# Sparse-expert stage on Trainium2: experts of two kinds taken in turn, with down products one expert behind

## The chip, the cores and the metric

The kernel runs on one core of a Trainium2 chip. The metric is the device time in microseconds (us) of one execution; several executions are timed and their median counts. A profile, taken by the hardware profiler, covers one execution.

The engines are PE (TensorE, matrix products; PEld is its loading of weights, which runs beside the products), DVE (VectorE), ACT (ScalarE), POOL (GpSimd) and SP (SyncE, which here issues most of the transfers).

## What is computed

A decoder of two layers for 256 tokens of 1024 channels in float32. Layer 1 ends with a SwiGLU of eight experts, of which each token uses two; the change lies there:

```python
logits = (xt @ w_router).astype(jnp.float32)
top_val, top_idx = lax.top_k(logits, TOP_K)          # 2 of 8
gates = jax.nn.softmax(top_val, axis=-1)
...
def expert_block(args):
    xb, e = args
    g, u = jnp.split(xb @ w_gate_up[e], 2, axis=-1)  # 1024 -> 2 x 3584
    return (jax.nn.silu(g) * u) @ w_down[e]          # 3584 -> 1024
```

The expert's rows, times their gates, are added to the residual. After it come a gated per-layer embedding and a last norm. The weights of one expert are 28 MiB for gate and up and 14 MiB for down, 44.04 MB in all; those of all eight, 352 MB, pass through once.

## The kernel before

**Precision.** A float32 product is made of products of two reduced parts: the high part of a tile is a copy in PE's reduced format, the low part the remainder. Every weight tile of 1 MiB that arrives is split so in two halves of 128 x 1024 by `wsplit`: ACT casts the high part `h_...` (line 145), DVE subtracts it and so makes the low part `l_...` (line 146). There are four buffers for each of the two (`SPL_BUFS`). `split` (lines 197 and 198) does the same for activations. All products are issued by `mm` (line 174).

**Two kinds of experts.** On the chip the experts are ranked by their number of tokens. The first four (ranks 0 to 3) have 128 slots: high and low tokens are separate tiles, and each piece of weights is used in three products of 512 columns, six for a half. The last four (`few(e)`, `FEW = 4`) have 64 slots: the high and low parts of their tokens stand side by side in one tile of 128 columns, so two products do, four for a half. Before, rank 0 comes first and rank 7 last.

**Chunks.** An expert's 3584 inner columns are taken in four chunks (`CHUNKS`), three of 1024 and one of 512. For each, `gate_up` makes the gate and up values in PSUM (`mg`, `mu`). `activate`, which `gate_up` returns, empties PSUM: for 128 slots ACT's Silu and DVE's product make the SwiGLU tile `msg` (lines 1191 and 1192); for 64 slots ACT copies both (`msg`, `msu`, line 1188). `h_T` then turns each tile of 512 columns on PE, since `down` needs the inner dimension on partitions: 128 slots by four transposes (line 1220) and a split into `mhh` and `mhl`; 64 slots by 16 small products with `both`, which add the low half to the high one at the same time (`mt`), after which Silu and product (lines 1211 and 1212) make `mgu` and a split makes `mh`. `down` adds the chunk's share to `y` in PSUM; after an expert's last chunk `combine` multiplies `y` with the slots' matrix and adds it to the residual `h` with the gates (line 1249).

**Order.** The loop at the end takes expert after expert and chunk after chunk. It issues `gate_up` of a chunk, then `back` of the chunk before. `h_T` of the chunk before is issued inside `gate_up`, at its second k tile (`MID = 1`), and `activate` of the present chunk after half of the `down` products (`between`). A scheduler fixes each engine's order from this order of issue; an engine then works strictly in its order. `gather` collects the tokens of two 128-slot experts, or of the four 64-slot ones, by products with a one-hot matrix; `spread_slots` turns that matrix for `combine`.

**Transfers.** Weights are requested on SP's queue in the order of use, into a ring of 11 buffers of 1 MiB (`raw`, `RAW_BUFS`; lines 766, 769 and 167), and for the first of them into two spare pairs of buffers (`SPARE`). A request waits until DVE has split what the buffer held. The weights of the last block (`r_dl`, line 1264) are split by output halves, so that the norm behind the stage can begin with the first half.

Of the kernel before, what the change touches and what calls it, by code (L numbers as in the profile page):

```python
# [16 lines left out]
P = 128  # L17
# [66 lines left out]
def trunk_kernel(  # L84
# [18 lines left out]
    def s2(name, shape, dt=F32):  # L103
        return ar.tile(list(shape), dt, tag="s2", name=name, bufs=S2_BUFS)

# [3 lines left out]
    def pt(name, shape=(P, 512)):  # L109
        return ps.tile(list(shape), F32, tag="t", name=name, bufs=2)  # L110
# [62 lines left out]
    def mm(o, a, b, start, stop, shared=False):  # L173
        last["mm"] = pe.matmul(o, a, b, start=start, stop=stop, skip_group_check=shared)  # L174
# [28 lines left out]
    def sub2(pr, *idx):  # L203
        return pr[0][idx], pr[1][idx]
# [738 lines left out]
    def layer1_moe(pT):  # L943
# [110 lines left out]
        def few(e):  # L1054
            return e >= FEW

# [141 lines left out]
        def h_T(e, c, sgs):  # L1198

            res = []  # L1200

            for i, sg in enumerate(sgs):
                if few(e):

                    q = pt(f"mt{e}{c}{i}", (P, 2, 4, P // 2))
                    for j in range(2):
                        for g in range(2):
                            for k in range(2):
                                mm(q[:, j, 2 * g + k, :], sg[j][:, 256 * g + k : 256 * g + 256 : 2], both, True, True)
                    t = s2(f"mgu{e}{c}{i}", [P, 4, P // 2])  # L1210
                    act.activation(t, q[:, 0], AF.Silu)
                    dve.tensor_tensor(t, q[:, 1], t, MUL)
                    hT = s2(f"mh{e}{c}{i}", [P, 4, 2, P // 2], F32R)
                    split((hT[:, :, 0], hT[:, :, 1]), t)
                    res += [hT[:, k].rearrange("q i s -> q (i s)") for k in range(4)]
                    continue
                q = pt(f"mt{e}{c}{i}", (P, 4, P))
                for g in range(2):
                    for k in range(2):
                        pe.transpose(q[:, 2 * g + k, :], sg[:, 256 * g + k : 256 * g + 256 : 2], ident)  # L1220
                hT = (s2(f"mhh{e}{c}{i}", [P, 4, P], F32R), s2(f"mhl{e}{c}{i}", [P, 4, P], F32R))
                split(hT, q)
                res += [sub2(hT, slice(None), k) for k in range(4)]
            return res

        def down(e, c, hT, yb, between):

            c0, n = CHUNKS[c]
            res = None
            for g in range(n // 256):  # L1230
# [3 lines left out]
                for i in range(2):  # L1234
                    products(e, [(yb[half], hT[2 * g + i], sub2(wt[i], slice(None), HALF[half])) for half in range(2)],
                             c == g == i == 0, c == len(CHUNKS) - 1 and g == n // 256 - 1 and i == 1)
                if g == n // 512 - 1 and between:
                    res = between()
            return res

        def combine(e, yb, half):
            s = slice(half * 512, half * 512 + 512)
# [8 lines left out]
        yb, hT = {}, {}  # L1251
        both = sm("both", (P, P // 2))
        dve.tensor_tensor(both, ident[:, : P // 2], ident[:, P // 2 :], ADD)

        def back(e, c, between=None):
            if c == 0:
                yb[e] = [py(f"y{e}{half}") for half in range(2)]
            if (e, c) == (NE - 1, len(CHUNKS) - 1):
                part = hT.pop((e, c))
# [11 lines left out]
            res = down(e, c, hT.pop((e, c)), yb[e], between)  # L1271
            if c == len(CHUNKS) - 1:
                for half in range(2):
                    combine(e, yb[e], half)
            return res

        def more_slots(e, pos):

# [58 lines left out]

            return over > P, more

        prev = None  # L1340
        for e in range(NE):
            for c in range(len(CHUNKS)):
                if e % 2 == 1 and c == 2 and e <= FEW - 1:
                    spread_slots = gather(e // 2 + 1)
                if (e, c) == (FEW, 1):
                    spread_slots()

                def mid():
                    if prev:
                        hT[prev] = h_T(*prev, sg)  # L1350
                    if (e, c) == (0, LATE):
                        for bn in todo:
                            product(*bn, pt)
                            copy(*bn)

                activate = gate_up(e, c, mid)
                if prev:
                    sg = back(*prev, activate)
                else:
                    sg = activate()  # L1360
                    with after("wsplit"):
                        gates()
                prev = e, c
        mid()
# [93 lines left out]
SPARE = ("gu0_0_0", "gu0_0_1", "d0_0_1", "d0_0_3", "d0_1_1", "d0_1_3", "d0_2_1", "d0_2_3", "d0_3_1", "d1_0_1", "d1_0_3")  # L1458
S2_BUFS = 12
SPL_BUFS = 4  # L1460
SPL_COLS = 1024
XT_BUFS = 2
# [30 lines left out]
```

## Time and profile before

| | |
|---|---|
| median of 3 runs | 1497.31 us (1495.36 to 1500.3) |
| the profiled execution | 1497.28 us, its span 1495.5 us |
| PE busy | 1444.5 us, 97% of the span |
| PEld busy | 1194.7 us, 80% |
| DVE busy | 1268.0 us, 85% |
| ACT busy | 1076.1 us, 72% |
| TensorE clock granted | 0.995 of full speed |
| DMA | 438.26 MB, mean 293 GB/s |

Busy times are sums over the whole span. Matmuls are pipelined and their ends are modelled, so a busy PE need not be a PE at its peak. The shares are averages over stages with different limits; the expert stage, some 900 us long, is the one that the change touches.

### The profile page before, as it was taken

To read this page: it belongs to the slowest core of one execution; us is meant where nothing else is said; L and a number is where in the kernel's file an instruction comes from. 1 tells how busy PE (TensorE), PEld (TensorE's weight loads), DVE (VectorE), ACT (ScalarE), POOL (GpSimd) and SP (SyncE) were. 2 spreads that over 40 slices of the span, in tenths; PEclk is the share of its full clock that TensorE was granted. 3 is DMA by queue.
4 is the path that set the end of the run, shared out by engine and by line. 5 is a ranking of instruction groups with operands and counts; after the bars stand their busy time and mean duration, and the time that the engine had idled before them with its cause. 6 is when DMAs were issued, how large, how long until landed. Compare 5 with 4: busy or idle time off the path is not lost.

```text
span 1495.5 us, 22012 instructions
## 1 busy us (share of the span) xinstructions
PE 1444.5 (97%) x7726; PEld 1194.7 (80%) x7726; DVE 1268.0 (85%) x1716; ACT 1076.1 (72%) x1441; POOL 4.9 (0%) x14
## 2 busy tenths in 40 slices
PE   7999999999999999999999999999999999999996
PEld 6999899988888878888888888886766666666665
DVE  6778655556698699999999989989999999999997
ACT  6545544446547678887887877779988988988975
POOL 0000000000000000000000000000000000000000
PEclk9999999999999999999999999999999999999998
DMA  9614656555452469898898998999999999999961
GB/s 350 241 43 131 216 177 196 172 195 185 147 203 106 149 248 354 327 410 333 322 376 336 392 347 341 359 363 389 377 409 414 390 413 410 388 413 408 394 254 44
DMA packets 136610, 438.26 MB, mean 293 GB/s; under 512 B 9067, under 2 KB 34188, under 8 KB 122412
## 3 DMA queue, kind: packets, MB, share of 16 engines
q1 hardware_dynamic: 132960, 433.19, 77.3%
q10 hardware_dynamic: 3148, 2.31, 0.5%
q0 software_dynamic: 384, 1.29, 0.4%
q8 instruction: 62, 1.02, 0.3%
q14 instruction: 56, 0.46, 0.1%
HBM read 434.92 MB, written 1.84 MB: 292 GB/s over the span
## 4 chain that ended last, share of the span: by engine, by line
PE 71%; DVE 18%; issue 4%; ACT 4%; DMA 3%; ACTq 0%; DVEq 0%; POOL 0%; POOLq 0%
PE y L174 14%; PE mg L174 11%; PE mu L174 11%; DVE l L146 11%; PE fu L174 4%; PE fg L174 4%; PE fd L174 4%; PE wo L174 3%; PE pg L174 3%; PE mt L174 2%; DMA r_gu<-in_moe_w_gate_up_dram 2%; DVE l_d L146 2%; PE p L174 1%; PE mt L1220 1%; PE in_og L174 1%
## 5 line engine op out<-in xcount | busy, mean ns | idle before, releaser
L146 DVE TENSOR_TENSOR l<-r_gu,h 128x1024 fp32r<-128x1024 f32 x448 | 526.3, 1218 | 18.1 <-ACT h L145 6.3
L145 ACT CAST h<-r_gu 128x1024 fp32r<-128x1024 f32 x448 | 456.6, 1052 | 60.2 <-PE mu L174 22.4
L146 DVE TENSOR_TENSOR l_d<-r_d,h_d 128x1024 fp32r<-128x1024 f32 x220 | 258.6, 1219 | 16.7 <-ACT h_d L145 10.4
L145 ACT CAST h_d<-r_d 128x1024 fp32r<-128x1024 f32 x220 | 226.8, 1054 | 24.7 <-PE mu L174 10.3
L146 DVE TENSOR_TENSOR l_gu<-r_gu,h_gu 128x1024 fp32r<-128x1024 f32 x44 | 53.8, 1224 | 47.7 <-ACT h_gu L145 47.7
L145 ACT CAST h_gu<-r_gu 128x1024 fp32r<-128x1024 f32 x44 | 46.0, 1048 | 64.2 <-PE fu L174 49.0
L174 PE MATMUL y<-l_d,mh 128*128 128x512 f32 x216 | 75.3, 430 | 3.7 <-DVE l_d L146 3.7
L174 PE MATMUL y<-l_d,mhh 128*128 128x512 f32 x224 | 69.8, 393 | 0.1
L174 PE MATMUL y<-h_d,mh 128*128 128x512 f32 x216 | 69.2, 402 | 0.3
L174 PE MATMUL y<-h_d,mhh 128*128 128x512 f32 x224 | 69.4, 391 | 0.0
L174 PE MATMUL y<-h_d,mhl 128*128 128x512 f32 x224 | 69.1, 390 | 0.0
L174 PEld LDWEIGHTS y<-l_d,mh 128*128 128x128 f32 x216 | 34.4, 188 | 27.4 <-DVE l_d L146 25.1
L146 DVE TENSOR_TENSOR l_fd<-r_fd,h_fd 128x1024 fp32r<-128x1024 f32 x22 | 26.9, 1224 | 27.3 <-ACT h_fd L145 26.3
L174 PE MATMUL fg<-x_ffn0h,h_gu 128*128 128x256 f32 x176 | 49.9, 283 | 0.0
L174 PE MATMUL fu<-x_ffn0h,h_gu 128*128 128x256 f32 x176 | 49.9, 283 | 0.0
L174 PE MATMUL fg<-x_ffn0h,l_gu 128*128 128x256 f32 x176 | 49.9, 283 | 0.0
L174 PE MATMUL fu<-x_ffn0l,h_gu 128*128 128x256 f32 x176 | 49.8, 283 | 0.0
L174 PE MATMUL fu<-x_ffn0h,l_gu 128*128 128x256 f32 x176 | 49.8, 283 | 0.0
L174 PE MATMUL fg<-x_ffn0l,h_gu 128*128 128x256 f32 x176 | 49.8, 283 | 0.0
L174 PEld LDWEIGHTS y<-h_d,mhl 128*128 128x128 f32 x224 | 42.1, 188 | 8.9
L174 PEld LDWEIGHTS y<-l_d,mhh 128*128 128x128 f32 x224 | 41.5, 188 | 9.5 <-DVE l_d L146 1.4
L174 PEld LDWEIGHTS y<-h_d,mhh 128*128 128x128 f32 x224 | 41.8, 188 | 8.9 <-ACT h_d L145 0.4
(719 smaller groups left out, 3673.6 us busy)
## 6 DMA issues: line engine op xcount, KB each, us to landing
r_gu<-in_moe_w_gate_up_dram SPq DMA_DIRECT2D x192, 1024.0 KB, 7.7
r_d<-in_moe_w_down_dram SPq DMA_DIRECT2D x110, 1024.0 KB, 7.7
r_gu<-in_moe_w_gate_up_dram SPq DMA_DIRECT2D x64, 512.0 KB, 6.4
r_gu<-in_ffn_w_gate_up_dram SPq DMA_DIRECT2D x44, 512.0 KB, 4.4
r_fd<-in_ffn_w_down_dram SPq DMA_DIRECT2D x11, 1024.0 KB, 4.9
r_wo<-in_ev_w_out_dram SPq DMA_DIRECT2D x4, 1024.0 KB, 12.8
r_pg<-in_ple_w_gate_dram SPq DMA_DIRECT2D x4, 1024.0 KB, 7.0
r_wo<-in_od_w_out_dram SPq DMA_DIRECT2D x4, 1024.0 KB, 5.0
```

The lines of the kernel that those rows point to most:

```text
L145: last["wcopy"] = act.copy(wh, raw[:, i : i + step])
L146: last["wsplit"] = dve.tensor_tensor(wl, raw[:, i : i + step], wh.bitcast(F32), SUB)
L174: last["mm"] = pe.matmul(o, a, b, start=start, stop=stop, skip_group_check=shared)
L1220: pe.transpose(q[:, 2 * g + k, :], sg[:, 256 * g + k : 256 * g + 256 : 2], ident)
```

## The change

- Experts are taken in the order 0, 4, 1, 5, 2, 6, 3, 7 (`ORDER`), a 128-slot one and a 64-slot one in turn.
- The `down` work of an expert is cut into blocks of 512 rows (2 MiB, four halves), and a list of blocks runs behind the list of gate and up chunks. A step (0 to 31) is one chunk of gate and up and the blocks after it: one block in steps 1 to 7 (`RAMP`), two from then on as far as they belong to one expert. So the blocks lag by about one expert, and a step's `gate_up` and `down` are mostly of different kinds. After step 31 three rounds of two 64-slot blocks remain, then the last block.
- `h_T` is cut up and issued at four k tiles of `gate_up` (`MIDS`): the turning of the chunk before, if it has 64 slots, at 1; its Silu and product (`turned`) at 3; the transposes of the step's 128-slot blocks (`across`) at 4; the split of the step's blocks at 6. SwiGLU values wait in `hidden` meanwhile, in 16 buffers instead of 12.
- `gather` of the 64-slot experts is at step 3, their `spread_slots` at 8, `gather` of experts 2 and 3 at 13.
- The embedding products `pj1`, made at step 1, go to DRAM by four transfers from ACT and come back by four on SP's queue, ahead of the last block's weights.
- The ring has 10 buffers, and `SPARE` names two tiles instead of eleven.

```diff
-        def gate_up(e, c, mid):
+        def gate_up(e, c, at):
...
             for k, j, wt in gate_up_weights(e, c):
-                if (k, j) == (MID, 0):
-                    mid()
+                if j == 0 and k in at:
+                    at[k]()
...
+        def turn(e, c):
             res = []
+            for i, sg in enumerate(hidden[e, c]):
+                q = pt(f"mt{e}{c}{i}", (P, 2, 4, P // 2))
...
+        def turned(e, c, banks):
+            t = s2(f"mgu{e}{c}", [P, len(banks), 4, P // 2])
+            for i, q in enumerate(banks):
+                act.activation(t[:, i], q[:, 0], AF.Silu)
+                dve.tensor_tensor(t[:, i], q[:, 1], t[:, i], MUL)
+            hidden[e, c] = t
+
+        def across(e, c, i):
+
+            if few(e):
+                return None
+            q = pt(f"mt{e}{c}{i}", (P, 4, P))
+            for g in range(2):
+                for k in range(2):
+                    pe.transpose(q[:, 2 * g + k, :], hidden[e, c][i][:, 256 * g + k : 256 * g + 256 : 2], ident)
+            return q
+
+        def h_T(e, c, i, q):
+
+            if few(e):
+                hT = s2(f"mh{e}{c}{i}", [P, 4, 2, P // 2], F32R)
+                split((hT[:, :, 0], hT[:, :, 1]), hidden[e, c][:, i])
+                return [hT[:, k].rearrange("q i s -> q (i s)") for k in range(4)]
+            hT = (s2(f"mhh{e}{c}{i}", [P, 4, P], F32R), s2(f"mhl{e}{c}{i}", [P, 4, P], F32R))
+            split(hT, q)
+            return [sub2(hT, slice(None), k) for k in range(4)]
...
-        prev = None
-        for e in range(NE):
-            for c in range(len(CHUNKS)):
...
+        gates_up = [(e, c) for e in ORDER for c in range(len(CHUNKS))]
+        downs = [(e, c, n) for e in ORDER for c in range(len(CHUNKS)) for n in range(CHUNKS[c][1] // 512)]
+        stored = dr.tile([P, NB, 2, 512], F32, name="pj1d")
+        fresh = None
+        while gates_up or len(downs) > 1:
+            now = gates_up.pop(0) if gates_up else None
+            step = NE * len(CHUNKS) - len(gates_up) - 1 if now else None
+            n = next((i for i, d in enumerate(downs) if d[:2] not in hidden), len(downs))
+            n = min(1 if now and step < RAMP else 2, n, sum(d[0] == downs[0][0] for d in downs))
+            blocks, downs = downs[:n], downs[n:]
+            if step == QUAD:
+                spread_slots = gather(2)
+            if step == SLOTS:
+                spread_slots()
+            if step == PAIR:
+                gather(1)
+            banks = {}
+
+            def turn_fresh():
+                if fresh and few(fresh[0]):
+                    banks["fresh"] = turn(*fresh)
...
+                    for b, i in BLOCKS:
+                        act.dma_start(stored[:, b, i], pj1[b][i])
...
+            if now:
+                activate = gate_up(*now, dict(zip(MIDS, (turn_fresh, fresh_turned, blocks_across, blocks_split))))
...
+            for i, d in enumerate(blocks):
+                back(*d, between if len(blocks) == 1 else None)
+                if i == 0 and len(blocks) == 2 and between:
+                    between()
...
         last_norm = halves_norm_T("ple1")
-        back(*prev)
+        for b, i in BLOCKS:
+            pj1[b][i] = s2(f"pj1{b}{i}", [P, 512])
+            sync.dma_start(pj1[b][i], stored[:, b, i])
+        hT[downs[0]] = h_T(*downs[0], across(*downs[0]))
+        back(*downs[0])
...
-RAW_BUFS = 11
+RAW_BUFS = 10
...
-MID = 1
+MIDS = (1, 3, 4, 6)
+RAMP = 8
+ORDER = (0, 4, 1, 5, 2, 6, 3, 7)
 FEW = 4
+QUAD, SLOTS, PAIR = 3, 8, 13
...
-S2_BUFS = 12
+S2_BUFS = 16
```

**First place: ACT, the down products of a step in which a 64-slot chunk of gate and up ends.** In these rows `h_d` is the high part of a down weight, `msg` and `msu` are the copies of gate and up, and `mgu<-mt` is the Silu of a turned tile. Before, the down weights are the same expert's:

```order
L1188 COPY msg_10362<-mg_10146 128x512 [waits PE_49]
L1188 COPY msu_10363<-mu_10148 128x512 [waits PE_49]
L1188 COPY msg_10366<-mg_10147 128x512
L1188 COPY msu_10367<-mu_10149 128x512 [waits PE_49]
L145 CAST h_d_0_2_0_10372<-r_d_0_2_10370 128x1024 [waits DMAHW6_49,DVE_49,PE_49]
L145 CAST h_d_0_2_1_10376<-r_d_0_2_10370 128x1024 [waits DVE_49,PE_49]
L1211 ACTIVATE mgu_10447<-mt_10438 128x256 [waits PE_49]
L145 CAST h_d_0_3_0_10390<-r_d_0_3_10388 128x1024 [waits DMAHW7_49,DVE_49]
L145 CAST h_d_0_3_1_10394<-r_d_0_3_10388 128x1024 [waits DVE_49]
L197 CAST mh_10450<-mgu_10447 128x4x64 [waits DVE_49]
L1211 ACTIVATE mgu_10462<-mt_10453 128x256 [waits PE_49,Activation_49]
```

After, they are a 128-slot expert's:

```order
L1189 COPY msg_10628<-mg_10406 128x512 [waits PE_49]
L1189 COPY msu_10629<-mu_10408 128x512 [waits PE_49]
L1189 COPY msg_10632<-mg_10407 128x512
L1189 COPY msu_10633<-mu_10409 128x512 [waits PE_49]
L145 CAST h_d_0_2_0_10638<-r_d_0_2_10636 128x1024 [waits DMAHW2_49,DVE_49,PE_49]
L145 CAST h_d_0_2_1_10642<-r_d_0_2_10636 128x1024 [waits DVE_49,PE_49]
L1215 ACTIVATE mgu_10766<-mt_10712 128x256 [waits PE_49]
L145 CAST h_d_0_3_0_10660<-r_d_0_3_10658 128x1024 [waits DMAHW3_49,DVE_49]
L145 CAST h_d_0_3_1_10664<-r_d_0_3_10658 128x1024 [waits DVE_49]
L145 CAST h_1_0_0_10686<-r_gu_1_0_10684 128x1024 [waits DMAHW4_49,DVE_49]
L145 CAST h_1_0_1_10690<-r_gu_1_0_10684 128x1024 [waits DVE_49,PE_49]
```

The Silu of the first turned tile keeps its place behind two casts and ahead of the next two. What moved is behind it: the `mh` cast of that tile and the Silu of the second are gone from these rows, into the next chunk's gate and up.

**Second place: DVE, from the last half of a 128-slot chunk's gate and up on.** `l_...` are low parts of gate and up weights, `l_d` of down weights, `msg` SwiGLU tiles. Before:

```order
L146 TENSOR_TENSOR l_0_7_1_6752<-r_gu_0_7_6745,h_0_7_1_6751 128x1024
L146 TENSOR_TENSOR l_d_3_0_0_6770<-r_d_3_0_6767,h_d_3_0_0_6769 128x1024
L146 TENSOR_TENSOR l_d_3_0_1_6774<-r_d_3_0_6767,h_d_3_0_1_6773 128x1024
L146 TENSOR_TENSOR l_d_3_1_0_6798<-r_d_3_1_6795,h_d_3_1_0_6797 128x1024
L1192 TENSOR_TENSOR msg_6789<-mu_6570,msg_6789 128x512
L1192 TENSOR_TENSOR msg_6792<-mu_6571,msg_6792 128x512
L146 TENSOR_TENSOR l_d_3_1_1_6802<-r_d_3_1_6795,h_d_3_1_1_6801 128x1024
L146 TENSOR_TENSOR l_1_0_0_6848<-r_gu_1_0_6845,h_1_0_0_6847 128x1024
```

After, where the down weights are a 64-slot expert's (its turned values have been in `mgu` for some time):

```order
L146 TENSOR_TENSOR l_0_7_1_9623<-r_gu_0_7_9616,h_0_7_1_9622 128x1024
L146 TENSOR_TENSOR l_d_0_0_0_9643<-r_d_0_0_9640,h_d_0_0_0_9642 128x1024
L146 TENSOR_TENSOR l_d_0_0_1_9647<-r_d_0_0_9640,h_d_0_0_1_9646 128x1024
L146 TENSOR_TENSOR l_d_0_1_0_9661<-r_d_0_1_9658,h_d_0_1_0_9660 128x1024
L146 TENSOR_TENSOR l_d_0_1_1_9665<-r_d_0_1_9658,h_d_0_1_1_9664 128x1024
L1193 TENSOR_TENSOR msg_9676<-mu_9432,msg_9676 128x512
L1193 TENSOR_TENSOR msg_9679<-mu_9433,msg_9679 128x512
L146 TENSOR_TENSOR l_d_0_2_0_9685<-r_d_0_2_9682,h_d_0_2_0_9684 128x1024
L146 TENSOR_TENSOR l_d_0_2_1_9689<-r_d_0_2_9682,h_d_0_2_1_9688 128x1024
L198 TENSOR_TENSOR mh_9864<-mgu_9049,mh_9864 128x4x64
L198 TENSOR_TENSOR mh_9867<-mgu_9049,mh_9867 128x4x64
```

The two `msg` products stand behind four halves of down weights instead of three; the remainders `mh` of the step's turned tiles have moved in among the down halves.

## Rows read from the trace of the kernel before

**Rows 1.** Timeline, DVE, 540 to 560 and 1440 to 1460 us: start, us, instruction, idle before.
```profile
552.82 1.29 DVE L1192 TENSOR_TENSOR msg<-mu,msg 128x512 f32<-128x512 f32 x2
...
1456.20 1.41 DVE L1249 SCALAR_TENSOR_TENSOR h<-cb,Gr,h 128x512 f32<-128x512 f32 x2 [0.92 <-PE cb L174]
```

**Rows 2.** Busy time by stretch; columns named in the first row.
```profile
core 0: us, PE busy (x) PEld busy (x) DVE busy (x) ACT busy (x) POOL busy (x), PEclk, DMA share, GB/s
675.60:800.00 124.40, 124.40 (x577) 103.22 (x577) 116.41 (x116) 99.45 (x110) 0.00 (x0) 1.00 0.93 347
800.00:920.10 120.10, 120.04 (x542) 99.28 (x541) 109.87 (x102) 93.64 (x100) 0.00 (x0) 1.00 0.96 364
1150.30:1259.50 109.20, 104.19 (x458) 73.61 (x456) 104.61 (x106) 95.14 (x115) 0.00 (x0) 1.00 1.02 405
```

**Rows 3.** Timeline, PE, 700 to 720 us, down products of a 128-slot expert.
```profile
700.95 0.62 PE L174 MATMUL y<-h_d,mhh 128*128 128x512 f32 x2
701.40 0.61 PE L174 MATMUL y<-h_d,mhl 128*128 128x512 f32 x2
701.85 0.62 PE L174 MATMUL y<-l_d,mhh 128*128 128x512 f32 x2
702.31 0.62 PE L174 MATMUL y<-h_d,mhh 128*128 128x512 f32 x2
```

**Rows 4.** Timeline, PE, 1300 to 1345 us, turning in a 64-slot expert.
```profile
1316.92 1.11 PE L174 MATMUL mt<-both,msu 128*128 128x64 f32 x8
1317.84 0.71 PE L174 MATMUL y<-l_d,mh 128*128 128x512 f32 x2
```

**Rows 5.** Timeline, DVE, 1120 to 1170 us, 64-slot experts.
```profile
1122.69 18.25 DVE L146 TENSOR_TENSOR l<-r_gu,h 128x1024 fp32r<-128x1024 f32 x16
...
1150.35 1.40 DVE L1249 SCALAR_TENSOR_TENSOR h<-cb,Gr,h 128x512 f32<-128x512 f32 x2
1151.67 0.67 DVE L198 TENSOR_TENSOR yl<-y,yh 128x512 fp32r<-128x512 f32 x1
1152.27 1.21 DVE L146 TENSOR_TENSOR l<-r_gu,h 128x1024 fp32r<-128x1024 f32 x1
...
1157.00 0.42 DVE L1212 TENSOR_TENSOR mgu<-mt,mgu 128x256 f32<-128x256 f32 x1
1157.34 2.35 DVE L146 TENSOR_TENSOR l<-r_gu,h 128x1024 fp32r<-128x1024 f32 x2
```

**Rows 6.** Waits, 1030 to 1440 us; SP's queue, 1040 to 1430: us, times, longest.
```profile
ACT mgu L1211 <- PE mt L174: 32.7, 18, 3.4
DVE l_d L146 <- ACT h_d L145: 9.1, 15, 0.9
DVE mgu L1212 <- ACT mgu L1211: 7.7, 11, 1.0
ACT h L145 <- DMA r_gu<-in_moe_w_gate_up_dram: 0.9, 2, 0.6
...
SPq L766 <- DVE l L146: 101.2, 54, 4.2
```

**Rows 7.** Timeline, ACT, 1300 to 1345 us.
```profile
1315.72 0.38 ACT L1211 ACTIVATE mgu<-mt 128x256 f32<-128x256 f32 x1 [1.99 <-PE mt L174]
1316.01 1.98 ACT L145 CAST h_d<-r_d 128x1024 fp32r<-128x1024 f32 x2
```

**Rows 8.** Timeline, DVE, 1300 to 1345 us.
```profile
1316.14 0.42 DVE L1212 TENSOR_TENSOR mgu<-mt,mgu 128x256 f32<-128x256 f32 x1 [0.57 <-ACT mgu L1211]
1317.08 2.36 DVE L146 TENSOR_TENSOR l_d<-r_d,h_d 128x1024 fp32r<-128x1024 f32 x2 [0.51 <-ACT h_d L145]
```

**Rows 9.** DMA, 1040 to 1430 us: total; issues with KB each and us to landing.
```profile
DMA packets 38405, 156.76 MB, mean 402 GB/s; under 512 B 2651, under 2 KB 2651, under 8 KB 31654
...
r_gu<-in_moe_w_gate_up_dram SPq DMA_DIRECT2D x80, 1024.0 KB, 8.6
```

**Rows 10.** Instructions by line and shape, 545 to 1495 us: busy, mean ns, idle.
```profile
L1220 PE MATMUL mt<-cst,msg 128*128 128x128 f32 x112 | 17.1, 281 | 0.0
```

**Rows 11.** The page's 40 slices of the span, DMA rate.
```profile
GB/s 350 241 43 131 216 177 196 172 195 185 147 203 106 149 248 354 327 410 333 322 376 336 392 347 341 359 363 389 377 409 414 390 413 410 388 413 408 394 254 44
```

More of the change, by code (lines that the diff above doesn't have):

```diff
@@ L1196, in gate_up @@
             return activate
-        def h_T(e, c, sgs):
+        def turn(e, c):
             res = []
[L1202 to L1223, printed above, removed]
-            return res
@@ L1226, in down @@
-        def down(e, c, hT, yb, between):
+            for i, sg in enumerate(hidden[e, c]):
+                q = pt(f"mt{e}{c}{i}", (P, 2, 4, P // 2))
+                for j in range(2):
+                    for g in range(2):
+                        for k in range(2):
+                            mm(q[:, j, 2 * g + k, :], sg[j][:, 256 * g + k : 256 * g + 256 : 2], both, True, True)
+                res.append(q)
+            return res
+        def turned(e, c, banks):
[4 more added lines that the diff above has]
+            hidden[e, c] = t
@@ new lines, in across @@
+        def across(e, c, i):
+            if few(e):
+                return None
+            q = pt(f"mt{e}{c}{i}", (P, 4, P))
+            for g in range(2):
+                for k in range(2):
+                    pe.transpose(q[:, 2 * g + k, :], hidden[e, c][i][:, 256 * g + k : 256 * g + 256 : 2], ident)
[8 more added lines that the diff above has]
+            return [sub2(hT, slice(None), k) for k in range(4)]
@@ L1228, in down @@
+        def down(e, c, i, hT, yb, between):
             c0, n = CHUNKS[c]
-            res = None
-            for g in range(n // 256):
+            for g in range(2 * i, 2 * i + 2):
                 nm = f"d{e}_{c}_{g}"
@@ L1233, in down @@
                 wt = wload(view, (2, D), nm, spare(nm))
[L1234 to L1239, printed above, removed]
+                for k in range(2):
+                    products(e, [(yb[half], hT[2 * (g % 2) + k], sub2(wt[k], slice(None), HALF[half])) for half in range(2)],
+                             c == g == k == 0, c == len(CHUNKS) - 1 and g == n // 256 - 1 and k == 1)
+                if g == 2 * i and between:
+                    between()
         def combine(e, yb, half):
@@ L1249, in combine, with back @@
                 dve.scalar_tensor_tensor(h[:, b, s], q, Gr[:, b, e : e + 1], h[:, b, s], MUL, ADD)
-        yb, hT = {}, {}
+        yb, hT, hidden = {}, {}, {}
         both = sm("both", (P, P // 2))
         dve.tensor_tensor(both, ident[:, : P // 2], ident[:, P // 2 :], ADD)
-        def back(e, c, between=None):
-            if c == 0:
+        def back(e, c, i, between=None):
+            if c == i == 0:
                 yb[e] = [py(f"y{e}{half}") for half in range(2)]
+            part = hT.pop((e, c, i))
             if (e, c) == (NE - 1, len(CHUNKS) - 1):
-                part = hT.pop((e, c))
                 rows = expert(moe_w_down, e)[CHUNKS[c][0] :].rearrange("(g q k) c -> g q k c", k=2, q=P)
@@ L1270, in back @@
                 return
-            res = down(e, c, hT.pop((e, c)), yb[e], between)
+            down(e, c, i, part, yb[e], between)
             if c == len(CHUNKS) - 1:
@@ L1338, in overflow @@
             return over > P, more
-        prev = None
-        for e in range(NE):
-            for c in range(len(CHUNKS)):
[L1343 to L1363, printed above, removed]
@@ L1364, in layer1_moe, with fresh_turned, blocks_across, blocks_split @@
-        mid()
-        last_norm = halves_norm_T("ple1")
-        back(*prev)
+        gates_up = [(e, c) for e in ORDER for c in range(len(CHUNKS))]
[18 more added lines that the diff above has]
+                    banks["fresh"] = turn(*fresh)
+                if now == (0, LATE):
+                    for bn in todo:
+                        product(*bn, pt)
+                        copy(*bn)
+                    for b, i in BLOCKS:
+                        act.dma_start(stored[:, b, i], pj1[b][i])
+            def fresh_turned():
+                if "fresh" in banks:
+                    turned(*fresh, banks["fresh"])
+            def blocks_across():
+                for d in blocks:
+                    banks[d] = across(*d)
+            def blocks_split():
+                for d in blocks:
+                    hT[d] = h_T(*d, banks[d])
+            if now:
+                activate = gate_up(*now, dict(zip(MIDS, (turn_fresh, fresh_turned, blocks_across, blocks_split))))
+                def between(now=now, activate=activate):
+                    hidden[now] = activate()
+            else:
+                for f in (turn_fresh, fresh_turned, blocks_across, blocks_split):
+                    f()
+                between = None
+            for i, d in enumerate(blocks):
+                back(*d, between if len(blocks) == 1 else None)
+                if i == 0 and len(blocks) == 2 and between:
+                    between()
+            if not blocks:
+                between()
+            if step == 0:
+                with after("wsplit"):
+                    gates()
+            fresh = now
@@ L1368, in layer1_moe @@
+        if fresh:
+            turned(*fresh, turn(*fresh))
+        last_norm = halves_norm_T("ple1")
+        for b, i in BLOCKS:
[3 more added lines that the diff above has]
+        back(*downs[0])
         return pj1, (last_norm[0], last_norm[2]()), overflow
```

3 lines of the change are left out of this document (1 added, 2 removed).

## The prediction

> **What bounds the kernel now.** I first looked for the stage in which the change works. The first product of gate and up values of the expert stage ends at 554.2 us (552.82 + 1.29), and the first sum of the last expert into the residual starts at 1456.20 [rows 1]. The change touches 902.0 us between these marks; everything outside stays as it is, apart from two small transfers.
>
> Then I read the busy time of each engine in three stretches, each from one expert's first sum to the next one's: four chunks of gate and up products, four of down products and one combine [rows 2]. The second is a plain 128-slot expert: PE is busy in 120.04 of its 120.10 us, DVE in 109.87, ACT in 93.64. **A 128-slot expert is bound by PE.** The third is a 64-slot expert: DVE 104.61 of 109.20, PE 104.19, ACT 95.14. To see which of the two is full there, I took PE's need from spacing instead of busy time. In a full stretch six products of one half (128 x 1024 weights, the unit in which they are split) start 1.36 us apart [rows 3], so 0.227 us a product; a 64-slot half has four, 0.91. Its 84 halves make 336 x 0.227 = 76.1 us, and its 112 turning products, 8 of which take 0.92 us [rows 4], another 12.9. With 8 products of combine, 1.8, that is 90.8 us. DVE takes 18.25 us for 16 halves, 1.14 each [rows 5]: 84 x 1.14 = 95.8, with 14 pairs of turned tiles (0.34 each for product and remainder) and combine's 3.9, 104.6 in all. **A 64-slot expert is bound by DVE**, and 4.6 us of its 109.2 are lost beside it.
>
> The waits of that stage say where [rows 6]. ACT waits 18 times, 32.7 us in all and 3.4 at most, for PE's turning; behind it DVE waits for ACT. One such place in order of time: ACT's Silu of a turned tile waits 1.99 us for PE, with two casts queued behind it [rows 7]; DVE then stands still for 0.57 and 0.51 us [rows 8]. Weights are not late: ACT waits for them 0.9 us in 400, and the SP queue is itself waiting for DVE to free buffers (101.2 us) [rows 6]. They arrive at 402 GB/s [rows 9].
>
> As a cross-check on busy time: PE's 104.19 us in the third stretch would make a 64-slot expert almost as PE-bound as DVE-bound, with a floor for a pair of 120.1 + 104.2 = 224.3 us; weight loading, 73.61 against 99.28 in the 128-slot one, scales to 73.61/99.28 x 120.1 = 89.0 and a floor of 209. The counted 90.8 agrees with the second. The Trainium skill ("Perfetto Trace Analysis", Identifying the Most-Contended Engine) says the same: pipelined products make busy time a bad measure, and weight-load busy time a good one.
>
> **The change part by part.** A pair (one expert of each kind) needs 211 us of PE (504 products, 114.2; 28 transposes at 0.153 [rows 10], 4.3; combine 1.8; and the 90.8) and 213 of DVE (95.8, seven SwiGLU products at 0.64 [rows 1], seven remainders at 0.60 and combine's 3.9 make 108.4; and the 104.6), and now takes 120.1 + 109.2 = 229.3. After the change each step runs gate and up products of one kind beside down products of the other. But only four split halves fit between DVE and PE, so phases overlap by little. I add them by hand.
>
> *128-slot step* (16 halves of gate and up, 8 light halves of down): PE bounds the first part, 16 x 1.36 = 21.8. DVE is 3 halves ahead when it ends; the other 5 take 5.7, two SwiGLU products (1.3) and two remainders of turned tiles (0.7) stand among them (second order listing), and 1.3 goes to the first wait and the last products: 9.0. Sum 30.8. The half-size fourth step: 8 x 1.36 + 4.2 = 15.1. With one turned tile (1.8) and combine on PE (1.8): 3 x 30.8 + 15.1 + 3.6 = **111.1**.
>
> *64-slot step* (16 light halves, then 8 heavy ones): DVE has 24 x 1.14 = 27.4, plus 0.7 for two turned products and 1.2 for two remainders. The first listing shows the Silu of the first turned tile still standing behind two casts and ahead of two: that wait is not removed. PE now spends 1.36 instead of 0.91 on each half ahead of it, so I put DVE's gap at 2.2 us, between 1.08 [rows 8] and the 3.4 of ACT's longest wait plus about 1 behind it [rows 6]; nearer the low end, because DVE has halves in hand. Sum 31.5; fourth step 8 x 1.14 + 4 x 1.36 + 0.5 = 15.0; combine on DVE 3.9, less 0.4 of product now elsewhere: 3 x 31.5 + 15.0 + 3.5 = **113.0**.
>
> A pair becomes 224.1 instead of 229.3. Three pairs in steady running (steps 8 to 31) save **15.6 us**.
>
> *The ends.* The rest now takes 902.0 - 3 x 229.3 = 214.1. After: steps 1 and 2, 128-slot with one block of 4 heavy halves, 21.8 + 5.4 + 0.6 (four transposes) = 27.8 each, and 1.3 for the late embedding products (675.6 - 554.2 = 121.4 for the first expert, against 120.1 [rows 1, 2]); step 3, 10.9 + 6.0 + 4.3 for a gather (the first stretch, which holds one: 124.4 against 120.1 [rows 2]) = 21.2; step 4, light gate and up by DVE, 18.2, then 5.4 on PE, 0.6 of transposes and 1.2 at the joints = 25.4; 5 and 6, DVE's 20 x 1.14 + 0.7 + 0.6 and the gap of 2.2 = 26.3 each; 7, 9.1 + 4.6 + 3.3 of combine = 17.0. That is 173.1. After the last step three rounds of two light blocks remain with nothing beside them, 24 x 1.14 + 6 x 0.34 + three starts of 1.5 = 34, then 7 for the last block's first half, 4.3 for the other gather and an estimated 0.4 for turning the slots: 218.8. **The ends cost 4.7 us.**
>
> *Edits at nothing.* One weight buffer less, and nine spare ones: ten 1 MiB buffers last DVE 23 us, and a transfer lands in 8.6 [rows 9]; uncovered, 2.6 us once. Storing the embedding products: 4 transfers from ACT 900 us before they are read. Reloading them: 1.05 MB on the SP queue ahead of the last weights, 2.6 us at 402 GB/s, hidden by what DVE still has to split; between 0 and 2.6, I take 0. More slots for small tiles: 0, they only remove waits.
>
> Sum: -15.6 + 4.7 = -10.9. The profiled execution took 1497.28 us, 0.03 below the median, so **1486.4, say 1486**. With a gap of 1.1 instead of 2.2 in 12 steps it is 13 less; with one half more or less ahead in 12 steps of the other kind, 14 either way. I do not expect all in one direction: its own range is 1478 to 1495.
>
> **Rivals.**
> *More overlap.* If PE keeps its queue so full that phases blend, a pair goes toward DVE's 213; 88.08 MB a pair at 402 GB/s allow 219. Three pairs at 214 to 219 give 1497.3 + 4.7 - 46 (or 31) = 1456 to 1471. For it: 211 and 213 of need are balanced. Against: four halves of 1.14 us are the only store, and phases last 9 to 22 us. Chance 0.20.
> *A larger wait of ACT* (slower). The Silu behind the two casts waits for turnings that PE reaches only between heavy products. If each wait leaves DVE idle for 4.7 us (3.4 + 1.3) instead of 2.2, 12 steps cost 30 more: 1516; it passes the old time from a gap of 3.1. For it: PE needs 1.5 times as long per half ahead of these turnings. Against: the waits in the trace cost DVE 1.08 us in [rows 8], and 0.9 + 1.0 = 1.9 at most by [rows 6]. Chance 0.18, with 1502 to 1516.
> *Weights become late.* The new pair asks 88.08 MB / 224.1 us = 393 GB/s all along. Slices of the light stage go down to 388 [rows 11]: 227.0 a pair, and 1495; with a pause in the ramp 1498. Against: ACT's 0.9 us of waiting at 402. Chance 0.12. The Trainium skill ("DMA: Bandwidth & Descriptors", Where 436 GB/s comes from) puts the limit of a core's reads from HBM near 358 GB/s; by that a pair would take 246 us and the kernel 1552. The trace contradicts it with 402 over 390 us, and I give that 0.01 at most, inside the 0.12.
>
> **How the numbers follow.** The forecast has 0.50. About 0.3%, 4.5 us, is what a measurement of this kernel can tell from no change: faster below 1492.8, slower above 1501.8. Of the forecast 0.41 lies below, 0.09 between; more overlap adds 0.20 to faster; late weights split into 0.02 faster and 0.10 the same; the larger wait gives 0.17 slower and 0.01 same. Faster 0.63, same 0.20, slower 0.17. The range leaves out the lower half of more overlap and the upper half of the larger wait: 1464 to 1508.
>
> **What would show it.** In the profile after: a 128-slot stretch near 111 us with PE full through gate and up, a 64-slot one near 113 with DVE busy some 95%; DVE's l_d waiting for ACT's casts behind mgu 2 to 3 us per 64-slot step; the ends 5 us longer, with PE under 80% busy in the last 34. Wrong if a pair stays at 229 or falls under 219, if ACT waits for r_gu or r_d more than a few us in all, or if SP waits for anything but DVE.

## The result, and the profile after

The change made the kernel slower: 1510.53 us median of 4 runs (1509.71 to 1512.87) against 1497.3 of 4, a ratio of 1.0089 with a 95% interval of 1.0069 to 1.0109. That is above the forecast's range (1464 to 1508), and on the other side of no change than the forecast. The profiled execution took 1512.87 us.

Busy time by stretch of the kernel after, with the columns of [rows 2]. The first row is the ramp; then come stretches from one expert's first sum to the next one's, each holding four steps whose gate and up products are of a 128-slot expert and of a 64-slot one in turn, the 128-slot one first; the 64-slot stretch from 840.6 us also holds a gather. The last row is what remains after the last step.

```profile
556.00:727.60 171.60, 168.78 (x796) 136.44 (x795) 158.91 (x159) 143.13 (x168) 0.00 (x0) 1.00 1.00 379
727.60:840.60 113.00, 109.82 (x480) 86.47 (x478) 108.72 (x106) 94.24 (x108) 0.00 (x0) 1.00 0.99 388
840.60:965.50 124.90, 119.23 (x563) 91.72 (x563) 111.11 (x116) 98.69 (x123) 0.00 (x0) 1.00 0.95 355
965.50:1077.20 111.70, 108.79 (x472) 85.84 (x470) 108.17 (x107) 91.78 (x102) 0.00 (x0) 1.00 1.00 394
1077.20:1198.10 120.90, 115.47 (x527) 87.67 (x527) 106.99 (x105) 95.02 (x114) 0.00 (x0) 1.00 0.97 367
1198.10:1309.70 111.60, 108.70 (x472) 85.77 (x470) 107.98 (x106) 91.69 (x102) 0.00 (x0) 1.00 1.00 392
1309.70:1430.60 120.90, 114.40 (x519) 85.95 (x518) 107.00 (x104) 95.02 (x114) 0.00 (x0) 1.00 0.97 371
1430.60:1472.10 41.50, 37.14 (x133) 25.86 (x133) 36.63 (x41) 29.12 (x36) 1.07 (x2) 0.88 0.70 250
```

Three of the four kinds came as forecast: ramp 171.6 us (173.1), 128-slot stretch 111.6 (111.1), remainder 41.5 (41). **The 64-slot stretch took 120.9 where 113.0 was forecast.** Its waits, from the wait view of that kernel (1077 to 1198 us; us, times, longest), answer to [rows 6], which span more than three and a half stretches:

```profile
ACT mgu L1215 <- PE mt L174: 17.9, 6, 4.1
...
DVE mgu L1216 <- ACT mgu L1215: 8.6, 4, 2.7
```

In the whole profile the group of the Silu now waits 69.7 us for PE's turning (last column of part 5 of the page), against 32.7 us in [rows 6] (36.0 in the whole profile before):

```profile
L1215 ACT ACTIVATE mgu<-mt 128x256 f32<-128x256 f32 x28 | 10.8, 385 | 69.7 <-PE mt L174 69.7
```

One 64-slot step in order of time, DVE, then ACT (timelines of the kernel after, 1095 to 1145 us; start, us, instruction, idle before). `mhh` and `mhl` are the high and low parts of a 128-slot tile that PE has transposed:

```profile
1097.50 6.89 DVE L146 TENSOR_TENSOR l_d<-r_d,h_d 128x1024 fp32r<-128x1024 f32 x6
1107.03 0.42 DVE L1216 TENSOR_TENSOR mgu<-mt,mgu 128x256 f32<-128x256 f32 x1 [2.63 <-ACT mgu L1215]
1107.97 2.36 DVE L146 TENSOR_TENSOR l_d<-r_d,h_d 128x1024 fp32r<-128x1024 f32 x2 [0.52 <-ACT h_d L145]
...
1114.85 0.42 DVE L1216 TENSOR_TENSOR mgu<-mt,mgu 128x256 f32<-128x256 f32 x1
1116.01 0.69 DVE L198 TENSOR_TENSOR mhl<-mt,mhh 128x512 fp32r<-128x512 f32 x1 [0.74 <-ACT mhh L197]
1116.96 2.36 DVE L146 TENSOR_TENSOR l<-r_gu,h 128x1024 fp32r<-128x1024 f32 x2 [0.26 <-ACT h L145]
...
1140.77 0.42 DVE L1216 TENSOR_TENSOR mgu<-mt,mgu 128x256 f32<-128x256 f32 x1 [2.67 <-ACT mgu L1215]
```

```profile
1106.61 0.38 ACT L1215 ACTIVATE mgu<-mt 128x256 f32<-128x256 f32 x1 [4.05 <-PE mt L174]
1106.89 1.99 ACT L145 CAST h_d<-r_d 128x1024 fp32r<-128x1024 f32 x2
...
1114.43 0.39 ACT L1215 ACTIVATE mgu<-mt 128x256 f32<-128x256 f32 x1 [1.76 <-PE mt L174]
1115.40 0.59 ACT L197 CAST mhh<-mt 128x512 fp32r<-128x512 f32 x1 [0.58 <-PE mt L1226]
```

From one first Silu product to the next is 1140.77 - 1107.03 = 33.7 us; 31.5 was forecast. DVE stands for 2.63 + 0.52 at the first tile and 0.74 + 0.26 behind the second, 4.15 us in all, where the forecast put 2.2. The 0.74 is a wait for ACT's cast `mhh`, which comes behind the second Silu and itself waits for PE's transposes. So far this is the rival "a larger wait of ACT". But PE is busy in 115.47 of the stretch's 120.9 us, and a gap of DVE is time only if DVE is the bound there. The experiments are about that.

### The profile page after: what moved, and what is told of

The parts are those of the page before. It is cut to its first block, busy times and chain, and to the rows that moved or that the text cites. A ratio compares the mean times of both kernels' runs of the same rounds, so it can differ in the third digit from the quotient of the medians.

```text
span 1511.1 us, 21970 instructions
## 1 busy us (share of the span) xinstructions
PE 1448.8 (96%) x7726; PEld 1201.3 (79%) x7726; DVE 1265.6 (84%) x1716; ACT 1067.3 (71%) x1441; POOL 5.0 (0%) x14
## 3 DMA queue, kind: packets, MB, share of 16 engines
q0 software_dynamic: 384, 1.29, 0.3%
## 4 chain that ended last, share of the span: by engine, by line
PE 70%; DVE 18%; ACT 5%; issue 4%; DMA 2%; ACTq 0%; DVEq 0%; POOL 0%; POOLq 0%
PE y L174 12%; PE mg L174 12%; PE mu L174 12%; DVE l L146 8%; PE fu L174 4%; PE fg L174 4%; PE fd L174 4%; DVE l_d L146 4%; PE mt L174 3%; PE wo L174 3%; PE pg L174 3%; PE p L174 1%; ACT h L145 1%; DMA r_gu<-in_moe_w_gate_up_dram 1%; PE pj L174 1%
## 5 line engine op out<-in xcount | busy, mean ns | idle before, releaser
L145 ACT CAST h<-r_gu 128x1024 fp32r<-128x1024 f32 x448 | 451.3, 1053 | 46.5 <-PE mu L174 22.5
L145 ACT CAST h_d<-r_d 128x1024 fp32r<-128x1024 f32 x220 | 223.7, 1055 | 22.3 <-PE mu L174 8.7
L1215 ACT ACTIVATE mgu<-mt 128x256 f32<-128x256 f32 x28 | 10.8, 385 | 69.7 <-PE mt L174 69.7
L174 PEld LDWEIGHTS y<-h_d,mh 128*128 128x128 f32 x216 | 41.4, 192 | 10.6 <-DVE mh L198 1.5
L174 PE MATMUL mu<-l,xe2l 128*128 128x512 f32 x112 | 40.9, 435 | 8.9 <-DVE l L146 8.1
```

The costliest lines, as they stand in the source:

```text
L145: last["wcopy"] = act.copy(wh, raw[:, i : i + step])
L1215: act.activation(t[:, i], q[:, 0], AF.Silu)
```

## The experiments

Each was timed together with the kernel before, whose median then lay between 1496.97 and 1497.46 us. Pin means that an instruction is ordered behind a named one on its engine.

| run | median us | ratio to before, 95% interval |
|---|---|---|
| pin_both | 1501.09 | 1.0026 (1.0016 to 1.0035) |
| pin_second | 1513.26 | 1.0106 (1.0089 to 1.0122) |
| delay_alone | 1525.44 | 1.0185 (1.0168 to 1.0202) |
| order_alone | 1494.35 | 0.9978 (0.9968 to 0.9988) |
| turn_late | 1495.02 | 0.9986 (0.9976 to 0.9996) |
| pin_six_buffers | 1487.08 | 0.9930 (0.9913 to 0.9946) |
| before_six_buffers | 1497.97 | 1.0004 (0.9995 to 1.0014) |
| before_pin | 1490.28 | 0.9952 (0.9935 to 0.9968) |
| late_six_buffers | 1475.57 | 0.9851 (0.9835 to 0.9868) |
| late_five_buffers | 1479.66 | 0.9879 (0.9863 to 0.9896) |
| order_pin | 1487.31 | 0.9932 (0.9916 to 0.9949) |
| order_pin_six | 1475.54 | 0.9854 (0.9838 to 0.9871) |

**pin_both: take ACT's wait out of the changed kernel.**

```diff
         def turned(e, c, banks):
             t = s2(f"mgu{e}{c}", [P, len(banks), 4, P // 2])
-            for i, q in enumerate(banks):
-                act.activation(t[:, i], q[:, 0], AF.Silu)
-                dve.tensor_tensor(t[:, i], q[:, 1], t[:, i], MUL)
+            with after("wcopy", "wsplit"):
+                for i, q in enumerate(banks):
+                    act.activation(t[:, i], q[:, 0], AF.Silu)
+                    dve.tensor_tensor(t[:, i], q[:, 1], t[:, i], MUL)
```

> The changed kernel, with the Silu and product of both turned tiles of a 64-slot chunk ordered behind the casts of the next chunk's fourth k tile. Theory A (the in-order wait): a 64-slot step of 33.7 us holds 4.17 us in which DVE stands still because ACT waits for PE's turning (2.65 + 0.52 at the first tile, 0.74 + 0.26 at the second). Without them DVE needs 29.5 and PE 30.3 to 30.8, so a step falls to about 30.6: 9 steps x 3.1 = 28, a few us more in the ramp; 1474 to 1486 us, the 64-slot stretch from 120.9 to 111 to 114. Theory B (PE is the bound of the step): PE is busy in 32.36 of the 33.7 us; DVE would only fill its four buffers earlier and then wait for PE. At most 1.3 us a step is to be had: 1497 us or more, the 64-slot stretch at 117 or more.

1501.09 us, 9.4 less than the change; the 64-slot stretch 117.5. That is theory B's answer (117 or more, 1497 or more), and not theory A's. In the stretch from 1073.3 to 1190.8 us ACT's wait for the turning was down from 17.9 to 1.4 us, so the edit did what it should. DVE's timeline of the run (1092 to 1142 us) shows what took its place:

```profile
1093.59 9.17 DVE L146 TENSOR_TENSOR l_d<-r_d,h_d 128x1024 fp32r<-128x1024 f32 x8
1103.75 1.23 DVE L146 TENSOR_TENSOR l<-r_gu,h 128x1024 fp32r<-128x1024 f32 x1 [1.00 <-ACT h L145]
1105.70 3.95 DVE L146 TENSOR_TENSOR l<-r_gu,h 128x1024 fp32r<-128x1024 f32 x3 [0.73 <-ACT h L145]
...
1125.96 9.16 DVE L146 TENSOR_TENSOR l_d<-r_d,h_d 128x1024 fp32r<-128x1024 f32 x8
```

DVE waits for ACT's casts again, and ACT, in its timeline of the same window, for PE to release a buffer:

```profile
1102.52 1.05 ACT L145 CAST h<-r_gu 128x1024 fp32r<-128x1024 f32 x1 [1.98 <-PE y L174]
1104.62 1.05 ACT L145 CAST h<-r_gu 128x1024 fp32r<-128x1024 f32 x1 [1.05 <-PE y L174]
```

In PE's timeline these two rows have a wait; the 56 rows between them have none:

```profile
1093.73 0.74 PE L174 MATMUL mu<-l,xe2l 128*128 128x512 f32 x2 [0.17 <-DVE l L146]
...
1120.96 0.73 PE L174 MATMUL mu<-l,xe2l 128*128 128x512 f32 x2 [0.25 <-DVE l L146]
```

PE is full for 27.2 of the 32.4 us of a step (1125.96 - 1093.59). In the other five it goes at DVE's pace: 16 products from 1120.96 to 1126.10, 0.32 us each, against 0.227 in a full row. The four buffers were full while DVE could have worked ahead. So of the 4.15 us per step 33.7 - 32.4 = 1.3 was time, as theory B had said.

**pin_second: the second tile alone.**

```diff
             for i, q in enumerate(banks):
+                with after("wcopy", "wsplit") if i else ExitStack():
...
```

> The same edit for the second tile alone; the first keeps its place behind two casts of down weights. Theory A: the first tile's 3.17 us of standing DVE stay, the second's 1.0 goes: 9 to 12 us less than the changed kernel at most, 1499 to 1506 us, and the wait of 4.05 us of ACT for the turning is still there once per step. Theory B: no difference beyond 2 us, 1508 to 1512.

1513.26 us: no gain; the 64-slot stretch 121.6. The 2.7 us more lie outside both expectations, but the intervals of the two ratios overlap (1.0089 to 1.0122, and 1.0069 to 1.0109 for the change). The run does not say what the 1.0 us behind the second tile is worth, since the edit left that wait in place and made it longer. DVE there had waited for the cast `mhh`; with the Silu out of its way ACT only comes to that cast sooner and waits for PE's transposes instead (DVE, 1075 to 1150 us, then ACT, 1095 to 1145 us):

```profile
1116.74 0.69 DVE L198 TENSOR_TENSOR mhl<-mt,mhh 128x512 fp32r<-128x512 f32 x1 [1.14 <-ACT mhh L197]
1117.69 2.36 DVE L146 TENSOR_TENSOR l<-r_gu,h 128x1024 fp32r<-128x1024 f32 x2 [0.26 <-ACT h L145]
```

```profile
1116.12 0.59 ACT L197 CAST mhh<-mt 128x512 fp32r<-128x512 f32 x1 [2.73 <-PE mt L1227]
```

DVE stands 1.14 + 0.26 = 1.40 us there instead of 1.00, and the step is 0.33 us longer (1141.82 - 1107.75 = 34.07, from one first Silu product to the next, against 33.74). DVE had done the second tile's product during that wait (0.42 us at 1114.85 in the rows of the change); now the product comes later, among light halves. In the two profiled executions the last expert's first sum comes 1.5 us later (1473.60 against 1472.13), mostly by the two plain 64-slot stretches, which are 0.7 us longer each.

**turn_late: PE's turning among light products.** The turning is pinned on PE too, and goes to the part of the step in which PE has time to spare; the transposes and the split of the step's blocks now stand ahead of it, and the Silu later than in pin_both.

```diff
+            with after("mm"):
...
-MIDS = (1, 3, 4, 6)
+MIDS = (5, 7, 1, 3)
```

> The run pin_both with the turning of a 64-slot chunk moved on PE behind the products of the next chunk's sixth k tile, its Silu and product to the eighth, and transposes and split of the blocks ahead of them (second and fourth). Theory B1 (PE's work stands in the wrong place): in pin_both PE is full for 26.4 of a step's 32.4 us, since 10.9 us of heavy down products, 3.7 of turning and 1.2 of transposes follow each other, and DVE stands with full buffers for 2.3 us; then PE waits for DVE. With the turning among light products, where PE needs 0.91 and DVE 1.14 us a half, a step falls towards 30.5: 64-slot stretch from 117.5 to 111 to 114, 1481 to 1491 us in all. Theory B2 (only the sum of PE's work counts): no change beyond 3 us, 1498 to 1504. Worse than 1506 if one block of 3.7 us of turning makes DVE's buffers run full by itself.

1495.02 us, 6.1 less than pin_both; the 64-slot stretch 114.0, and PE is free of turning while it has heavy products. A step is now 31.5 us (from 1123.49 to 1154.97, the starts of two steps' down products on DVE). The total lies between theory B1's range (1481 to 1491), which had put 30.5 for a step, and that of B2 (1498 to 1504); the 6.1 us are twice what B2 allowed. So where PE's work stands counts, and not its sum alone. How much of it the turning brings and how much the transposes, split and Silu that moved with it was not tried apart. The products are the same; busy time by stretch of pin_both, and then of turn_late, from one 64-slot stretch each:

```profile
1073.30:1190.80 117.50, 112.98 (x527) 87.97 (x527) 107.70 (x105) 95.45 (x114) 0.00 (x0) 1.00 0.99 380
```

```profile
1072.40:1186.40 114.00, 111.60 (x527) 88.80 (x527) 106.19 (x105) 95.60 (x114) 0.00 (x0) 1.00 1.00 394
```

**Two halves of the change by themselves.** delay_alone has the experts in the order 0 to 7:

```diff
-ORDER = (0, 4, 1, 5, 2, 6, 3, 7)
+ORDER = (0, 1, 2, 3, 4, 5, 6, 7)
...
-QUAD, SLOTS, PAIR = 3, 8, 13
+QUAD, SLOTS, PAIR = 14, 17, 6
```

> The changed kernel with the experts in the order 0 to 7, so that down products still lag by an expert but stand beside gate and up products of the same kind except at one border. Theory A: in 64-slot steps the turning now stands between light down products (0.91 us a half instead of 1.36), so ACT's wait is as short as in the kernel before; 128-slot steps have none. Pairs as before the change, 229 us, plus 5 us of ends: 1498 to 1506 us. If the wait were set by the delay itself (turning beside another expert's down products), it stays at 4 us per 64-slot step and the time is above 1510.

1525.44 us, above the 1510 that was to speak for the delay itself, though not for the reason given: ACT's longest wait for the turning in a 64-slot stretch is 3.1 us (1213.7 to 1328.4), not 4. The 64-slot stretch rose from 109.1 to 114.7, since both Silus of a chunk now stand together among the down products (DVE, 1235 to 1270 us), and DVE is the bound there:

```profile
1241.26 0.42 DVE L1216 TENSOR_TENSOR mgu<-mt,mgu 128x256 f32<-128x256 f32 x1 [0.57 <-ACT mgu L1215]
1243.60 0.42 DVE L1216 TENSOR_TENSOR mgu<-mt,mgu 128x256 f32<-128x256 f32 x1 [1.92 <-ACT mgu L1215]
1244.54 2.36 DVE L146 TENSOR_TENSOR l_d<-r_d,h_d 128x1024 fp32r<-128x1024 f32 x2 [0.52 <-ACT h_d L145]
```

That is 3.0 us a chunk against 1.08 in [rows 8], 16 us in three stretches. The other 12 are the ends: expert 0's first sum comes 58 us later, and what follows expert 6's takes 41.5 instead of 87.6, 46 less.

order_alone is the kernel before with the kinds in turn, and the changed kernel's buffers:

```diff
-        for e in range(NE):
+        for e in ORDER:
...
-RAW_BUFS = 11
+RAW_BUFS = 10
...
+ORDER = (0, 4, 1, 5, 2, 6, 3, 7)
...
-S2_BUFS = 12
+S2_BUFS = 16
```

(`gather(2)` moves to chunk 3 of expert 0, `gather(1)` to chunk 1 of expert 5, `SPARE` as in the change.)

> The kernel before with the experts in the order 0, 4, 1, 5, 2, 6, 3, 7, ring, spare and small buffers as in the changed kernel, down products one chunk behind as before. Steps keep their kind, so every stretch keeps its length apart from borders between kinds: 1494 to 1502 us. Slower than 1505 would mean that taking the kinds in turn (or the smaller ring) costs time by itself.

1494.35 us, 3 less than before, as expected. So the change's loss is not in taking the kinds in turn, nor in the ring of 10.

**before_pin: the wait where DVE is the bound.**

```diff
-                    act.activation(t, q[:, 0], AF.Silu)
-                    dve.tensor_tensor(t, q[:, 1], t, MUL)
+                    with after("wcopy", "wsplit"):
+                        act.activation(t, q[:, 0], AF.Silu)
+                        dve.tensor_tensor(t, q[:, 1], t, MUL)
```

> The kernel before with Silu and product of each turned tile ordered behind the casts of the next chunk's second k tile. 64-slot stretches are bound by DVE there, so each 1.1 to 1.6 us that DVE stands behind ACT's wait is time: 14 chunks x 1.1 to 1.6 = 15 to 22 us less, 1475 to 1484, the 64-slot stretch from 109.2 towards 105.5. If PE were the bound of that stage too, as it was in the changed kernel, less than 5 us.

1490.28 us, 6.8 less, between the two answers: the stretch of a 64-slot expert falls from 109.1 to 107.5. Even there the buffers run full: ACT's casts wait for PE to release one, 5.3 us in one 64-slot stretch (1145 to 1255 us), a wait that the view of the kernel before does not have:

```profile
ACT h L145 <- PE y L174: 5.3, 5, 1.3
```

**The store between DVE and PE.** The edit of the runs with other buffers is of this kind; the sizes of the ring are in the expectations:

```diff
-RAW_BUFS = 10
+RAW_BUFS = 8
...
-SPL_BUFS = 4
+SPL_BUFS = 6
```

> The run pin_both with six buffers each for high and low halves instead of four, paid with two buffers of the ring (8 instead of 10). If the four halves between DVE and PE are what keeps phases of PE and phases of DVE from overlapping, a 128-slot step loses about 2 halves of DVE, 2.3 us, and a 64-slot step comes near PE's 30.5: 12 x 2.3 + 9 x 1.9 = 40 less at most, and weights at 402 GB/s then allow no pair below 219: 1465 to 1480 us. If the halves are not it, 1498 to 1504. If eight buffers in the ring are too few, ACT waits for weights and the time is above 1504.

> The kernel before with six buffers for high and low halves and a ring of 9. Stretches of one kind have the same bound throughout, so a longer store between DVE and PE changes little: DVE's gaps at the turning (about 1.1 us a chunk of a 64-slot expert) stay, since DVE is the bound there: 1491 to 1499 us. A gain over 10 us would mean that the store, and not the mixing of kinds, is what counts.

pin_six_buffers 1487.08 us, 14.0 less than pin_both. The 128-slot stretch went from 111.6 to 108.4; the 64-slot one stayed at 117.6. There ACT, which runs further ahead, stands in its queue again: it waits 4.1 us for PE's turning and 9.8 for its transposes (1062.6 to 1180.3 us), against 1.4 and 4.9 in pin_both. The store is a limit, though 40 us was far too much. before_six_buffers 1497.97: nothing, as expected. The reason is argued from the order of ACT's queue: while the Silu stands ahead of the casts, ACT cannot fill buffers that are free. What bears it out is order_pin_six below, where the Silu is out of the way and the buffers do help; its experts are in another order, though.

> The run turn_late with six buffers for high and low halves and a ring of 8. If the place of PE's turning and the four halves of store each cost by themselves, both gains add: 128-slot stretch 112.3 to 109, 64-slot stretch 114.0 to 110 to 112, three pairs 16 to 22 us less and a little in the ramp: 1473 to 1480 us. If they are one cause (either gives DVE the room that the turning took), it stays near the better of the two, 1485 to 1489. If weights become late at 88.08 MB per 220 us = 400 GB/s, ACT's wait for transfers grows past 10 us and the time lies between.

> The same with five buffers and a ring of 9. If the store is what counts, about half of the gain of six over four: 1483 to 1488 us when six gives 1473 to 1480, and a 128-slot stretch near 110.7. If only the sixth counts, or none, 1494 or the same as six.

1475.57 and 1479.66 us: six buffers give the time that was expected if the gains of turn_late (6.1) and pin_six_buffers (14.0) add, and rather more than the sum, 25.5 below pin_both; five were expected to give half of the gain and gave 15.4 of 19.5. One 64-slot and one 128-slot stretch of late_six_buffers:

```profile
1062.10:1174.80 112.70, 110.69 (x527) 89.08 (x527) 106.13 (x104) 94.92 (x114) 0.00 (x0) 1.00 1.02 407
1174.80:1283.20 108.40, 107.20 (x472) 86.27 (x470) 106.61 (x107) 90.28 (x102) 0.00 (x0) 1.00 1.00 393
```

**Is the delay worth its ends?** order_pin is order_alone with the edit of before_pin; order_pin_six adds the six buffers.

> The run order_alone (kinds in turn, no delay) with Silu and product of each turned tile ordered behind the casts of the next chunk's second k tile. In stretches of one kind DVE is the bound of 64-slot chunks, so the wait is time, as in before_pin (6.8 us): 1486 to 1490 us. Then the delay, which needs longer ends, has to gain 7 us more than that to be worth its place.

> The run order_pin with six buffers for high and low halves and a ring of 8: kinds in turn, no delay. Without the delay each step's gate and up and its down products are of the same kind, so phases of PE and of DVE last a whole expert (110 us) and two more halves can shift only about 2 us at each of 7 borders, of which the gain is PE's or DVE's slack there: 1482 to 1488 us, against 1475.6 for the delayed kernel with the same buffers. If it reaches 1478 or less, the delay gains nothing even with six buffers.

1487.31 us, as expected, and 1475.54: a miss of mine, 6.5 us below its range, and the same time as late_six_buffers. The two added buffers cut ACT's wait for PE to release one, in one 64-slot stretch, from 5.3 us to 1.1. The wait row of order_pin (1133.6 to 1244.2 us), then of order_pin_six (1126.9 to 1234.6):

```profile
ACT h L145 <- PE y L174: 5.3, 5, 1.3
```

```profile
ACT h L145 <- PE y L174: 1.1, 1, 1.1
```

The 64-slot stretches of order_pin_six fall to 107.7, the 128-slot ones stay at 116.7 and full of PE:

```profile
1010.20:1126.90 116.70, 115.42 (x507) 91.94 (x506) 107.24 (x103) 89.92 (x103) 0.00 (x0) 1.00 0.99 383
1126.90:1234.60 107.70, 105.99 (x492) 82.02 (x491) 105.40 (x107) 92.50 (x113) 0.00 (x0) 1.00 1.02 402
```

A pair is 224.4 us without the delay and 221.1 with it. The delay does overlap the kinds, by 3.3 us a pair, 10 in three (with the turning moved, which order_pin_six does not have). Its ends cost as much: the first sum comes 54.5 us later (726.59 against 672.05), and what follows the last but one expert's first sum is only 43.3 shorter (40.26 against 83.52). Both versions are 1.5% faster than the kernel before, and the one without the delay is the simpler.

## Why the prediction was wrong

- **The failed step is the 64-slot step of 31.5 us**, "DVE has 24 x 1.14 = 27.4 ...", with its gap "at 2.2 us". Measured were 33.7 us. In the sum's own terms DVE's work was right (busy 29.55 us from 1107.0 to 1140.7, against 27.4 + 0.7 + 1.2 = 29.3), and **the gap was mis-sized**: 4.15 us, between the ends that I had given (1.08 and 4.4), near the upper. The argument for the lower end, that DVE has halves in hand, did not hold.
- The sum also had the wrong form: it cost DVE's work alone and laid the wait on top. With the wait pinned away a step is still 32.4, since PE is full for 27.2 of them: heavy down products, turning and transposes follow each other there, which I had counted over an expert (211 us a pair) but not where they stand. With the turning also moved it is 31.5. Over a stretch: 120.9, 117.5 and 114.0 against 113.0 forecast, so 3.4 us for the wait, 3.5 for PE's work in the wrong place, 1.0 left.
- By the forecast's own sum a gap of 4.15 instead of 2.2 in 12 steps makes 1486.4 + 23.4 = 1509.8, nearly what was measured. That is luck: with the waits pinned away only 1.3 of the 4.15 us of a step went, and the ramp, which was to hold some of the 12 gaps, was 1.5 us shorter than forecast.
- Nearly all of the miss lies in the 64-slot stretches. The stage was forecast 10.9 us shorter than before; it came from 902.0 to 916.2 (555.9 to 1472.13), 25 more than forecast. Two 64-slot stretches give 7.9 each; the one with a gather, 124.9 against 113.0 + 4.3, another 7.6; the 128-slot stretches 2.6 (with the 0.4 for turning the slots in the first), ramp and remainder -1.0.
- Right: the 128-slot stretch (111.6 against 111.1); the ends as a cost; weights were not late (ACT waited for them 0.3 us in the ramp and not at all from 727 to 1430 us). SP still waited for DVE. The lead in the 128-slot step was smaller than the three halves assumed: when PE ended its heavy products, at 1220.95 us, DVE had split two and begun the third, and the light part took 9.3 us (to 1230.24) instead of 9.0. A sign that failed: PE was to be under 80% busy in the last 34 us, and was 32.79 of 35.00, 94%, from 1437 to 1472. "More overlap" was rightly held back by the four halves of store: with six the 128-slot stretch gained 3.2 us.
- The rival "a larger wait of ACT" gave 1502 to 1516, and the time fell there. Its mechanism was in the trace and its price was not: the wait itself was 9.4 of the 24 us between forecast and result, as far as pin_both takes it out. That a pinned Silu would leave PE as the bound, neither the forecast nor that rival had.
- On busy time as a floor: the cross-check chose 90.8 us of counted products over 104.19 of busy time. For a pair this held, since late_six_buffers runs it in 221.1, below the 224.3 that busy time would have as floor. It says how much PE needs, not when.
- Slips in the working that change nothing: 552.82 + 1.29 makes 554.1, not 554.2; a 64-slot expert has 7 pairs of product and remainder at 0.34 each, not 14, which makes 104.5 of DVE; and the upper end of the gap is 4.4 in the step and 4.7 in the rival.

Left open: the wait for the transposes behind the second tile was in no run taken out by itself, and the detour of the embedding products through DRAM and the length of the ramp were not tried apart.

## What to carry to other kernels

When work of two kinds is to share a step, lay both engines' work along the step, in the order of their queues, and let neither run ahead by more than the buffers between them; sums over a stage say only what is possible. A gap on an engine is worth its length only where that engine is the bound, so before fixing a wait ask which engine is full behind it. An instruction that waits in an in-order queue can also make added buffers useless: take the wait out first, then add buffers, and look again, since an engine that runs further ahead comes sooner to the next instruction that waits.

## What was not expected of the hardware

The same 527 products of a 64-slot stretch show PE busy for 115.47 us in the changed kernel, 112.98 in pin_both, 111.60 in turn_late and 110.69 in late_six_buffers, all at a granted clock of 1.00, while weight loading lies between 87.67 and 89.08. So the busy time that the profile gives for PE fell with the length of the stretch, and not with the work. The Trainium skill ("Perfetto Trace Analysis", Identifying the Most-Contended Engine) calls the busy share of matmuls a poor measure of how near a kernel is to its limit, and names the busy share of weight loads instead, beside the share of peak arithmetic. These runs agree: PE's share was 115.47 / 120.9 = 96% in the changed kernel, where 8.2 us were still to be had, while that of weight loads was 87.67 / 120.9 = 73% and rose to 89.08 / 112.7 = 79%.
